# A decoder step in float32: all of the sample's mLSTM state updates moved off TensorE into the MLP, part of them on ScalarE and GpSimd

## The chip, the core and the metric

The kernel runs on one core of a Trainium2 chip. The metric is the device time of one execution in microseconds. The engines are TensorE (PE in the profile, its weight loads PEld), VectorE (DVE), ScalarE (ACT), GpSimd (POOL) and the sync engine (SP), from whose queue nearly all DMAs are started.

## The reference

One layer of a decoder for 320 tokens: a prompt of 256 and a sample of 8 sequences with 8 tokens each (`NP_`, `NB`, `NT`). Two token mixers, an xLSTM mLSTM with 4 heads and an HGRN2 with 8, share one input projection; then come the gates, an output projection, a LayerNorm and an MLP of 2048 to 8192 to 2048 with a squared ReLU. What matters here is the new mLSTM state of each of the 8 sample sequences, an output of 4 heads x 256 x 512 per sequence:

```python
C_new = decay[..., None, None] * C + jnp.einsum('bhs,bhsk,bhsv->bhkv', w_end, kc, vc)
```

So a state row k of a sequence is scaled by one number and receives eight outer-product terms, one for each token s: a scalar (weighted key) times a row of 512 values. The old state C is also read for the output, `einsum('bhtk,bhkv->bhtv', qc, C)`.

## The kernel before

**Weights and TensorE.** Each of some 300 weight tiles (2048 rows x 128 columns) is read in two units of 128 x 1024 numbers. A unit is loaded into `wr` (three buffers, 512 KB each), ScalarE rounds it to the high half `wh`, VectorE subtracts to get the low half `wl`, and TensorE multiplies each of its 8 blocks three times (high x high, high x low, low x high) with 320 columns of activations: 24 matmuls a unit. There are three `wh`/`wl` buffers, and in some stages five more in `bb`. The tiles follow in a fixed order: the mLSTM heads, the HGRN2 heads, gates and branches, `w_out`, and then four rounds of 16 `up` and 16 `dn` tiles of the MLP, which take the last 900 us.

**The order of everything else.** The program is written by a small scheduler (`Sched`). Each piece of work is a generator (a chain) that yields requests such as `("dve", cost, fn)`, `acq` and `rel` for buffers, `wait` and `post` for events. The scheduler keeps a clock per engine out of costs written in the code and puts an instruction on its engine's queue when the clock says that it would be ready. On the chip each queue runs strictly in the order so found. The kind `"bg"` is for background work on VectorE: it is issued only when VectorE's clock is at most 250 ns ahead.

**The sample's states.** For every head, `m_states` loads sixteen pieces of 128 state rows x 512 values (8 sequences x 2 halves of the keys) into `cb` buffers. `m_sample` makes two groups of them. A group first does some small sums (`m_few`), whose results ScalarE copies out of PSUM, then eight products of queries and states. For the first half of the key rows, `m_sums` multiplies `kst` and `vst` (the sample's weighted keys and values, spread over four row groups by broadcast loads and split into high and low parts) into four PSUM banks, one sequence each; `m_update` adds them on VectorE to the scaled state, and `m_store` writes it back.

The second half of the key rows is updated late, in the MLP, when the five buffers in `bb` are given up at the twelfth `up` tile (`retire`). `m_late` reads, for each head, the values of the eight tokens (`vsD`, broadcast to 16 partitions per sequence), the weighted keys (`kD`) as scalars per partition, and the decay (`scr`). A partition is a sequence and one of 16 blocks of 8 key rows; a piece (`m_late_part`) is two of the eight rows, 128 x 1024 values, loaded again from `C0`. ScalarE scales a piece by the decay, then VectorE does 16 operations (8 tokens x 2 rows) of the kind state = value row x key scalar + state, each 128 x 512, and the piece is stored. Four pieces a head, one head after the other, all in a tile called `fu`. When the last head is done, `late_end` gives the space to the prompt's final states (`m_C`), whose loads stand on GpSimd's queue.

Of the kernel before, what the change touches and what calls it, by code (L numbers as in the profile page):

```python
# [8 lines left out]
F32 = mybir.dt.float32  # L9
# [142 lines left out]
class Sched:  # L152
    PE_SIDE = 900.0
    BG = 250.0

# [17 lines left out]
    def step(self, c, now):  # L173
# [27 lines left out]
        else:  # L201
# [6 lines left out]
            if kind == "bg":  # L208
                if (r > now and c.eng != kind) or self.t["dve"] > now + self.BG:
# [11 lines left out]
            end = self.use("dve" if kind == "bg" else kind, r, cost)  # L221
# [86 lines left out]
class Program:  # L308
# [49 lines left out]
    def carve(self):  # L358
# [39 lines left out]
        self.kst = Pool([R.three(2, 128)])  # L398
        self.vst = Pool([R.three(2, 512)])
# [515 lines left out]
    def m_start(self, h):  # L915
# [19 lines left out]
        for name, evs, pool in (("qk", ("dn", "KS", "QW"), self.qk), ("eb", ("N", "S0"), self.eb), ("shl", ("N", "S0"), self.shl),  # L935
                                ("vhl", ("N",), self.vhl), ("vs", ("S0", "vst"), self.vs), ("kst_", ("QW", "KS"), self.kst), ("vst_", ("QW", "vst"), self.vst)):
# [98 lines left out]
    def m_Vs(self, h):  # L1035
# [6 lines left out]
        vst = yield acq(self.vst)  # L1042
        m["vst_"] = vst
        yield from self.sample_rows(self.vtD[h][:, NP_:TOK], vs, vst, self.khl, m["Vs"], m["vst"])

    def sample_rows(self, of, vs, vst, pool, both, four):
# [6 lines left out]
        for j in range(n):  # L1053
# [8 lines left out]
        yield wait(d)  # L1062
        for g in range(2):
# [30 lines left out]
    def m_KW(self, h):  # L1094
# [29 lines left out]
        kst = yield acq(self.kst)  # L1124
        m["kst_"] = kst
        yield from self.fourfold(self.kD[h][256:320, 0:128], kst)
        t = yield acq(self.khl)
        yield from self.high_low(kst.rearrange("p g k -> p (g k)"), t[:, 0:256], 0)
        yield rel(self.khl, t)
# [127 lines left out]
    def m_sample(self, h):  # L1257
# [18 lines left out]
        for k in range(2):  # L1276
# [119 lines left out]
    def m_done(self, h, name, evs, pool):  # L1396
# [3 lines left out]
        if name in ("kst_", "vst_"):  # L1400
            yield wait(*m["inter"])
# [22 lines left out]
    def m_sums(self, h, n, ps):  # L1424

        m = self.mh[h]
        kst, vst = m["kst_"], m["vst_"]
        g = self.state(n)[0] // 4
        for x in range(4):
            self.mm(ps[x], kst[32 * x:32 * x + 32, g, :], vst[32 * x:32 * x + 32, g, :], start=True, stop=True)  # L1430

    def m_update(self, h, n, cbs, ps):

        v, m = self.nc.vector, self.mh[h]
        b = self.state(n)[0]
        for x in range(4):
            yield post(m["inter"][n + 4 + x])
            yield rel(self.cb, cbs[4 + x])
        for x in range(4):
            cb, p, bx = cbs[x], ps[x], b + x  # L1440
            t = yield ("dve", dve(512, True, 1, 1), lambda: v.scalar_tensor_tensor(cb, cb, m["bc"][:, 704 + bx:705 + bx], p, ALU.mult, ALU.add))
            self.s.spawn(self.m_store(h, n + x, cb), 3, t)
            yield rel(self.sbank, p)

    def m_store(self, h, n, cb):
        m = self.mh[h]
        yield ("sp", 620, lambda: self.dma(self.d["Cs"][h, 0, self.state(n)[0]], cb))
        yield post(m["inter"][n])
        yield wait(self.later(2500))
        yield rel(self.cb, cb)  # L1450

    def retire(self, now, hl):

        self.spare.append(hl)
        if len(self.spare) == len(self.wx):
            A = self.Part(self.pool.tile([128, 10240], F32, name="fu", tag="f1"))
            self.lv, self.lc, self.lk = (Pool([]) for _ in range(3))
            self.lv.free = [(now, A.three(4, 512)) for _ in range(2)]
            self.lc.free = [(now, A(1024)) for _ in range(5)]
            self.lk.free = [(now, A(80)) for _ in range(2)]  # L1460
# [3 lines left out]
    def m_late(self, h):  # L1464

        if h:
            yield wait(self.late_ev[h - 1])
        v = yield acq(self.lv, 2)
# [3 lines left out]
        yield ("sp", 620, lambda: self.dma(k[:, 64:65], at(self.scr[h, 704:712].unsqueeze(1))))  # L1472
        for t in range(NT):
            yield wait(self.later(1500))
            x = self.kD[h][NP_:TOK, 128:256].rearrange("(b t) (d r) -> t b d r", t=NT, r=8)[t]
            yield ("sp", 620, lambda: self.dma(k[:, 8 * t:8 * t + 8], x))
        for i in range(4):
            yield wait(self.later(5000))
            x = self.vsD[h].rearrange("(b t) n -> b (t n)", t=NT)[:, 1024 * i:1024 * i + 1024]
            yield ("sp", 620, lambda: self.dma(v[i // 2][:, 2 * (i % 2):2 * (i % 2) + 2, :].rearrange("p t n -> p (t n)"), at(x)))  # L1480
        e = self.later(12000)
        evs = [Ev() for _ in range(4)]
        for q, x in enumerate(evs):
            self.s.spawn(self.m_late_part(h, q, v, k, e, x), 9, e.t + 8000.0 * q - 7000.0)
        yield wait(*evs)
        for x in v:
            yield rel(self.lv, x)
# [976 lines left out]
```

## Time and profile before

| | |
|---|---|
| time, median of three runs | 2244.96 us (2244.36 to 2246.15) |
| the profiled execution | 2246.38 us |
| its span, first to last instruction | 2244.6 us |
| granted TensorE clock | 0.999 |
| busy: PE, PEld, DVE, ACT, POOL | 2236.5, 2208.9, 1583.6, 1029.5, 21.1 us |
| DMA, mean over the span | 200 GB/s |

Rows of groups read: line, engine, operation, tiles written <- tiles read, shapes, count, then busy time in us, mean duration of one in ns, and the idle time of the engine just before them with what ended it. Timeline rows read: start in us from the span's start, busy us, engine and instruction, with the idle time ahead of it in brackets. The names in the profile leave out buffer numbers: `ra` holds `kst` and `vst`, `f` and `rx` the `cb` buffers and more, `bank` a PSUM bank. L352 is the helper that issues all matmuls, L346 the one for all ScalarE operations, L1512 the late update.

### The profile page before, as it was taken

The numbers are of one execution on the slowest core, as the hardware profiler recorded it, in microseconds if no ns is written. First come the engines' busy times: TensorE is split into PE (matmuls) and PEld (weight loads), VectorE is DVE, ScalarE is ACT, GpSimd is POOL, SyncE is SP. The second block draws the span as 40 slices with busy tenths as digits, with TensorE's granted clock in tenths as the row PEclk, the third lists the DMA queues.
The fourth block names the chain that finished last, engine by engine and source line by source line (L and its number), as shares of the span: only waits on it lengthen the run. The fifth ranks groups of instructions, "written<-read, shape, count | busy, mean of one in ns | idle before, by whom it ended". The sixth has DMA issues, their size and how long they took to land.

```text
span 2244.6 us, 40808 instructions
## 1 busy us (share of the span) xinstructions
PE 2236.5 (100%) x16186; PEld 2208.9 (98%) x16186; DVE 1583.6 (71%) x2808; ACT 1029.5 (46%) x1543; POOL 21.1 (1%) x53
## 2 busy tenths in 40 slices
PE   9999999999999999999999999999999999999999
PEld 9999999999999999999999999999999999999998
DVE  6757667789888887666555778368595885944575
ACT  5445445455555565444434456233443444334444
POOL 0000000000000000000000000000000000000000
PEclk9999999999999999999999999999999999999999
DMA  7987987777778765555556544375656657554654
GB/s 247 293 242 242 247 252 232 208 225 214 218 232 236 216 191 176 174 173 172 174 173 217 182 147 153 112 229 181 208 196 180 214 185 210 187 194 150 211 171 148
DMA packets 293145, 449.50 MB, mean 200 GB/s; under 512 B 141508, under 2 KB 187856, under 8 KB 292952
## 3 DMA queue, kind: packets, MB, share of 16 engines
q1 hardware_dynamic: 291992, 443.73, 63.4%
q0 software_dynamic: 960, 3.15, 0.4%
q8 instruction: 127, 2.08, 0.4%
q14 instruction: 66, 0.54, 0.1%
HBM read 397.44 MB, written 49.87 MB: 199 GB/s over the span
## 4 chain that ended last, share of the span: by engine, by line
PE 99%; DMA 0%; ACT 0%; DVE 0%; issue 0%; SPq 0%; DVEq 0%
PE bank L352 99%; DMA f<-xw 0%; ACT wh L346 0%; ACT f L346 0%; SPq L355 0%; ACT misc L346 0%; DVE wh L779 0%; DVE f L2130 0%; DVE f3m L2305 0%; DVE f2l L2129 0%; DVE oS L1896 0%; ACT oS L346 0%; DVEq L1896 0%
## 5 line engine op out<-in xcount | busy, mean ns | idle before, releaser
L346 ACT ACTIVATE wh<-wr 128x1024 fp32r<-128x1024 f32 x563 | 596.6, 1060 | 886.9 <-PE bank L352 789.3
L523 DVE TENSOR_TENSOR wl<-wr,wh 128x1024 fp32r<-128x1024 f32 x563 | 688.1, 1222 | 354.0 <-ACT wh L346 347.4
L352 PE MATMUL bank<-xh,wl 128*128 128x320 f32 (+1 forms) x2896 | 894.6, 310 | 0.0
L352 PE MATMUL bank<-xh,wh 128*128 128x320 f32 (+1 forms) x2896 | 893.5, 309 | 0.5 <-DVE wh L779 0.5
L352 PE MATMUL bank<-xl,wh 128*128 128x320 f32 (+1 forms) x2896 | 890.8, 309 | 0.0
L352 PEld LDWEIGHTS bank<-xh,wh 128*128 128x128 f32 x2896 | 544.2, 188 | 3.8 <-issue 2.0
L352 PEld LDWEIGHTS bank<-xl,wh 128*128 128x128 f32 x2896 | 543.8, 188 | 1.9
L352 PEld LDWEIGHTS bank<-xh,wl 128*128 128x128 f32 x2896 | 545.2, 188 | 0.0
L352 PE MATMUL bank<-ra,wh 128*128 128x320 f32 x1728 | 470.9, 308 | 0.0
L352 PE MATMUL bank<-rxb,wh 128*128 128x320 f32 x1024 | 315.7, 308 | 0.0
L352 PE MATMUL bank<-rxb,wl 128*128 128x320 f32 x1024 | 315.6, 308 | 0.0
L352 PEld LDWEIGHTS bank<-ra,wh 128*128 128x128 f32 x1728 | 309.9, 188 | 0.0
L352 PEld LDWEIGHTS bank<-rxb,wl 128*128 128x128 f32 x1024 | 192.2, 188 | 0.0
L352 PEld LDWEIGHTS bank<-rxb,wh 128*128 128x128 f32 x1024 | 192.2, 188 | 0.0
L1512 DVE SCALAR_TENSOR_TENSOR fu<-fu 128x512 f32<-128x512 f32 x256 | 179.9, 749 | 0.0
L352 PE MATMUL bank<-bb,wh 128*128 128x320 f32 x512 | 112.6, 309 | 0.0
L352 PE MATMUL bank<-ra,wl 128*128 128x320 f32 x352 | 108.5, 308 | 0.0
L346 ACT ACTIVATE f<-bank 128x320 f32<-128x320 f32 (+3 forms) x86 | 33.9, 394 | 114.6 <-PE bank L352 113.6
L352 PEld LDWEIGHTS bank<-bb,wh 128*128 128x128 f32 x512 | 85.5, 188 | 0.0
L346 ACT ACTIVATE f<-f,misc 128x320 f32<-128x320 f32 x136 | 76.2, 560 | 7.0 <-DVE f L2286 3.8
L352 PE MATMUL bank<-bb,wl 128*128 128x320 f32 x256 | 79.1, 309 | 0.0
L346 ACT ACTIVATE f<-f 128x320 f32<-128x320 f32 (+1 forms) x138 | 62.3, 452 | 16.2 <-DVE f L2291 12.3
(345 smaller groups left out, 1916.0 us busy)
## 6 DMA issues: line engine op xcount, KB each, us to landing
wr<-wt SPq DMA_DIRECT2D x602, 512.0 KB
rx<-C SPq DMA_DIRECT2D x34, 256.0 KB
fu<-vsD SPq DMA_DIRECT2D x16, 512.0 KB
fu<-C SPq DMA_DIRECT2D x16, 512.0 KB
Cs<-fu SPq DMA_DIRECT2D x16, 512.0 KB
f<-C SPq DMA_DIRECT2D x30, 256.0 KB
Cs<-f SPq DMA_DIRECT2D x16, 256.0 KB
Cs<-rx SPq DMA_DIRECT2D x16, 256.0 KB
```

The source lines that it names most:

```text
L346: return self.nc.scalar.activation(out, in_, func, **kw)
L352: self.nc.tensor.matmul(*a, **kw)
L523: self.V().tensor_tensor(lo, raw, hi.bitcast(F32), ALU.subtract)
L1512: yield ("bg", dve(512, False, 1, 1), lambda: self.nc.vector.scalar_tensor_tensor(cb[:, r], x, y, cb[:, r], ALU.mult, ALU.add))
```

## The change

The first half of the key rows is no longer updated in the mLSTM stage: `m_sums`, `m_update`, `m_store`, `kst` and `vst` go, with the loads and splits that feed them. The group on TensorE ends after its products with the states, the small sums get a bank of their own, and the group no longer waits for `kst` and `vst`. Instead `m_late` makes eight pieces per head, four for each half of the keys. Pieces 1, 3 and 5 are done without VectorE: ScalarE writes value row x key scalar into one of three buffers (`lp`), and GpSimd adds it to the state. A new kind `"bga"` holds back such ScalarE work as `"bg"` does on VectorE. There are three value buffers (half a head each) instead of two, so a piece may begin when the first four tokens' values are there, four piece buffers instead of five, and the next head starts its loads as soon as the last one's have been issued. The head's first four pieces are spaced only for head 0; otherwise the scheduler fits them in where its clocks allow.

```diff
+    LOW = dict(bg="dve", bga="act")
...
-            yield wait(m["KS"], m["vst"], m["S"])
+            yield wait(m["S"])
             dn = yield acq(self.sm)
-            ps = yield acq(self.sbank, 4)
-            t = yield ("pe", PE_C + PE_4 + pe_r(512) + 200.0, lambda: (
-                self.m_few(m, k, ps[3], dn, self.qn0[:, lo:lo + 128]), [self.mm(
+            p = yield acq(self.sbank)
+            yield ("pe", PE_C + 200.0, lambda: (
+                self.m_few(m, k, p, dn, self.qn0[:, lo:lo + 128]), [self.mm(
...
-                start=k == 0 and c == 0, stop=False, skip_group_check=True) for c in range(2) for x in range(4)], self.m_sums(h, 8 * k, ps)))
-            self.s.spawn(self.m_update(h, 8 * k, cbs, ps), 3, t)
+                start=k == 0 and c == 0, stop=False, skip_group_check=True) for c in range(2) for x in range(4)]))
+            yield rel(self.sbank, p)
...
-            self.lv.free = [(now, A.three(4, 512)) for _ in range(2)]
-            self.lc.free = [(now, A(1024)) for _ in range(5)]
+            self.lv.free = [(now, A.three(4, 512)) for _ in range(3)]
+            self.lc.free = [(now, A(1024)) for _ in range(4)]
+            self.lp.free = [(now, B(512)) for _ in range(3)]
...
+                for q in range(8):
+                    s.spawn(self.m_late_part(h, q, v, k, got, half[q], done[q]), 9, now + 6000.0 * q if h == 0 and q < 4 else now)
...
+        yield ("bga", act(1024, False, 1), lambda: self.A(buf, buf, scale=k[:, 128:129]))
...
+                if q % 2 and q < 6:
+                    p = yield acq(self.lp)
+                    yield ("bga", act(512, False, 1), lambda: self.A(p, x, scale=y))
+                    evs.append(Ev())
+                    self.s.spawn(self.m_late_add(cb[:, r], p, evs[-1]), 9)
+                else:
+                    yield ("bg", dve(512, False, 1, 1), lambda: self.nc.vector.scalar_tensor_tensor(cb[:, r], x, y, cb[:, r], ALU.mult, ALU.add))
...
+    def m_late_add(self, x, p, ev):
+
+        yield ("pool", 1000, lambda: self.nc.gpsimd.tensor_tensor(x, x, p, ALU.add))
+        yield rel(self.lp, p)
+        yield post(ev)
```

How the order moves is shown at three places. First, TensorE at the first state group of head 0, before (`misc<-` in a bank's row are the small sums, `f_79` and `rx` the states, `ra` with 512 columns the products of `kst` and `vst`, the other rows weight matmuls):

```order
L352 MATMUL bank_83<-xh,wl 128x320
L352 MATMUL bank_86<-misc,f_78 32x1 x8
L352 MATMUL bank_86<-f_76 32x32 x4
L352 MATMUL bank_87<-f_79 32x512 x6
L352 MATMUL bank_87<-rx,f_79 32x512 x2
L352 MATMUL bank_89<-ra 128x512
L352 MATMUL bank_90<-ra 128x512
L352 MATMUL bank_85<-ra 128x512
L352 MATMUL bank_86<-ra 128x512
L352 MATMUL bank_83<-xh,wh 128x320
```

The same place after the change:

```order
L353 MATMUL bank_83<-xh,wl 128x320
L353 MATMUL bank_89<-misc,f_78 32x1 x8
L353 MATMUL bank_89<-f_76 32x32 x4
L353 MATMUL bank_87<-f_79 32x512 x6
L353 MATMUL bank_87<-rx,f_79 32x512 x2
L353 MATMUL bank_83<-xh,wh 128x320
```

The four products are gone, of which the last wrote the bank of the small sums (`bank_86`); the group stands 72 rows earlier, and so it goes at all eight groups.

Second, VectorE in the MLP, while a head's late update runs, before (`wl<-wr,wh` is the split of a weight unit, `fu<-fu` the late update, the 320-wide rows are evacuations of the MLP's tiles):

```order
L523 TENSOR_TENSOR wl<-wr,wh 128x1024
L1512 SCALAR_TENSOR_TENSOR fu<-fu 128x512 x4
L523 TENSOR_TENSOR wl<-wr,wh 128x1024
L1512 SCALAR_TENSOR_TENSOR fu<-fu 128x512
L2291 SCALAR_TENSOR_TENSOR f_78<-bank_84,f2l 128x320
L1512 SCALAR_TENSOR_TENSOR fu<-fu 128x512 x2
```

And after:

```order
L522 TENSOR_TENSOR wl<-wr,wh 128x1024
L1488 SCALAR_TENSOR_TENSOR fu<-fu,f_78 128x512 x3
L522 TENSOR_TENSOR wl<-wr,wh 128x1024
L1488 SCALAR_TENSOR_TENSOR fu<-fu,f_78 128x512
L2297 TENSOR_TENSOR f3m<-f3m,bank_87 128x320
L1488 SCALAR_TENSOR_TENSOR fu<-fu,f_78 128x512 x2
```

The pattern is the same, three late rows a unit. What moved is how long it lasts: before, stretches of this kind (some 20 units, one per head) alternate with stretches without late rows, from unit 396 to unit 532 of 602; after, it runs without a break from unit 398 to unit 502, 320 rows instead of 256.

Third, ScalarE at the same time after the change, with the semaphores that each row waits for (before, its rows there are weight splits `wh<-wr`, evacuations and one `fu<-fu 128x1024` per piece):

```order
L347 ACTIVATE wh<-wr 128x1024 [waits DMAHW3_49,DVE_49,PE_49]
L347 ACTIVATE f_78<-fu,f_78 128x512 [waits Pool_49] x4
L347 ACTIVATE wh<-wr 128x1024 [waits DMAHW6_49,DVE_49,PE_49]
L347 ACTIVATE f_78<-fu,f_78 128x512 [waits Pool_49] x4
L347 ACTIVATE wh<-wr 128x1024 [waits DMAHW1_49,DVE_49,PE_49]
L347 ACTIVATE f_78<-fu,f_78 128x512 [waits Pool_49] x3
```

Up to four products now stand between two weight splits, and each waits until GpSimd has added the product that held its buffer. GpSimd's queue has one row for all of them, `TENSOR_TENSOR fu<-fu,f_78 128x512 x192`, ahead of the loads for `m_C`.

More of the change, by code (lines that the diff above doesn't have):

```diff
@@ L220, in step @@
                 return False
-            end = self.use("dve" if kind == "bg" else kind, r, cost)
+            end = self.use(self.LOW.get(kind, kind), r, cost)
             fn()
@@ L1052, in sample_rows @@
         e = self.later(5000)
-        for j in range(n):
+        for j in range(n if vst is not None else 0):
             for g in range(2):
@@ L1061, in sample_rows @@
         yield post(both)
-        yield wait(d)
-        for g in range(2):
+        if vst is not None:
+            yield wait(d)
+        for g in range(2 if vst is not None else 0):
             yield from self.high_low(vst[:, g, :], t[:, 0:128 * n], 1)
```

123 lines of the change are left out of this document (51 added, 72 removed).

## Prediction

> **What bounds the kernel now.** I read the page's totals first, then the chain that ended last, then the stages.
>
> ```profile
> span 2244.6 us, 40808 instructions
> PE 2236.5 (100%) x16186; PEld 2208.9 (98%) x16186; DVE 1583.6 (71%) x2808; ACT 1029.5 (46%) x1543; POOL 21.1 (1%) x53
> ...
> PE 99%; DMA 0%; ACT 0%; DVE 0%; issue 0%; SPq 0%; DVEq 0%
> ```
>
> TensorE (PE) works in 2236.5 of 2244.6 us, and the chain is 99% TensorE. So two things alone can move the time: TensorE instructions that vanish, and TensorE made to wait. Everything else is covered, as long as the cover lasts. Whether it lasts is read by stage (columns: PE, PEld, DVE, ACT, POOL busy us and count, clock, DMA share, GB/s):
>
> ```profile
> 1500.00:1550.00 50.00, 50.00 (x342) 50.00 (x342) 49.85 (x69) 16.44 (x16) 0.00 (x0) 1.00 0.58 197
> ...
> 90.00:400.00 310.00, 308.99 (x2203) 293.41 (x2200) 208.07 (x409) 144.96 (x235) 0.00 (x0) 1.00 0.82 244
> ```
>
> In the MLP, where one head of the late states is being updated, VectorE is already full (49.85 of 50 us) without TensorE losing anything; 342 matmuls in 50 us are 0.1462 us each. ScalarE is a third busy, GpSimd idle. The average of 71% for VectorE hides this.
>
> **What leaves TensorE.** These are timeline rows of TensorE at three of the eight state groups, in the mLSTM stage (start, us, instruction):
>
> ```profile
> 90.20 0.50 PE L352 MATMUL bank<-ra 32*128 32x512 f32 x3
> 91.33 0.50 PE L352 MATMUL bank<-ra 32*128 32x512 f32 x1 [0.64 <-ACT misc L346]
> 91.76 0.41 PE L352 MATMUL bank<-xh,wh 128*128 128x320 f32 x1
> ...
> 99.86 0.51 PE L352 MATMUL bank<-ra 32*128 32x512 f32 x4
> 100.30 0.41 PE L352 MATMUL bank<-xh,wh 128*128 128x320 f32 x1
> ...
> 178.62 0.50 PE L352 MATMUL bank<-ra 32*128 32x512 f32 x3
> 179.49 0.49 PE L352 MATMUL bank<-ra 32*128 32x512 f32 x1 [0.37 <-ACT misc L346]
> ```
>
> The four 32-row products of a group run side by side: from the first of them to the next weight matmul 100.30 - 99.86 = 0.44 us, and 8 x 0.44 = 3.5 us. At two groups the fourth product also waits until ScalarE has copied the small sums out of the same bank: 91.33 - 90.20 = 1.13 and 179.49 - 178.62 = 0.87 us, 2.0 us together. After the change the small sums have a bank of their own and nothing follows in it. So TensorE gains 5.5 us; the bounds are 3.5 (the copies delay something else) and 5.5. The 32 PSUM updates on VectorE, twelve high/low passes on each of ScalarE and VectorE, and 40 broadcast loads leave the same stage; VectorE has 102 us free there and TensorE waits about 1 us in all, so I cost them at nothing. The groups of head 0 now come some ten microseconds earlier; their state loads move up with them, since the broadcasts that stood between them on the sync queue are gone. I cost that at nothing (bounds: 0, and one late load of about 1 us, as the waits above).
>
> **What comes into the MLP.** Per head eight pieces instead of four. From the order: 320 products-and-sums on VectorE instead of 256, 32 ScalarE scalings instead of 16, and new: 192 ScalarE products with 192 GpSimd additions. All of it stands between the weight splits of units 398 and 503, where before it reached unit 532. That is 105 units of 24 matmuls, 2520 x 0.1462 = 368.4 us of TensorE. VectorE's rows:
>
> ```profile
> L1512 DVE SCALAR_TENSOR_TENSOR fu<-fu 128x512 f32<-128x512 f32 x256 | 179.9, 749 | 0.0
> ...
> L2305 DVE TENSOR_TENSOR f3m<-f3m,bank 128x320 f32<-128x320 f32 x36 | 17.5, 486 | 15.4 <-PE bank L352 15.0
> ```
> ```profile
> 1505.61 2.07 DVE L1512 SCALAR_TENSOR_TENSOR fu<-fu 128x512 f32<-128x512 f32 x3
> 1507.60 1.22 DVE L523 TENSOR_TENSOR wl<-wr,wh 128x1024 fp32r<-128x1024 f32 x1
> 1508.74 0.75 DVE L1512 SCALAR_TENSOR_TENSOR fu<-fu 128x512 f32<-128x512 f32 x1
> ```
>
> Durations overlap, so the step from start to start is what counts when VectorE is full: (1507.60 - 1505.61)/3 = 0.663 us, 1.14 us for a weight split, and by the same 0.085 us of overlap 0.40 us for a 320-wide row. In the stretch: 320 x 0.663 = 212.2, 105 x 1.14 = 119.7, 81 x 0.40 = 32.4, together 364.3 us of 368.4. It fits, with 4 us to spare over the whole stretch, where before the same stretch held 276 us. What lead there is beyond that shows in the longest wait of ScalarE's split for a free buffer:
>
> ```profile
> ACT wh L346 <- PE bank L352: 790.0, 407, 5.4
> ```
>
> About 5 us. So VectorE can lose 4 + 5 = 9 us in this stage before TensorE stands still, and with the 5.5 us gained, 14.5 us before the kernel is slower than it was. Spread over 192 additions this is 0.075 us each. That number decides the sign.
>
> ScalarE: 192 products; the nearest row, with a scale per partition and 512 columns, has 718 ns.
>
> ```profile
> L346 ACT ACTIVATE ra<-ra,cst 128x512 fp32r<-128x512 f32 x12 | 8.6, 718 | 1.7 <-DVE ra L1143 1.7
> ...
> L346 ACT ACTIVATE fu<-fu 128x1024 f32<-128x1024 f32 x16 | 18.2, 1139 | 0.3 <-DMA fu<-C 0.2
> L346 ACT ACTIVATE wh<-wr 128x1024 fp32r<-128x1024 f32 x563 | 596.6, 1060 | 886.9 <-PE bank L352 789.3
> ```
>
> 192 x 0.72 = 138, 32 x 1.14 = 36, 105 x 1.06 = 111 and 56 evacuations of 0.5, 28: 313 of 368 us. It fits by itself, but ScalarE takes its queue in order, and behind each product that waits for one of three GpSimd buffers stands the next weight split. Transfers: 16 loads and 16 stores of 512 KB more, in 370 instead of 476 us, make (80 x 0.524 MB)/370 us = 113 GB/s instead of 53: 197 + 60 = 257 GB/s, near the 244 at a share of 0.82 that cost TensorE 1 us in 310. Nothing, bound 3 us. The 64 short key loads instead of 32 and the 32 large transfers add some 64 issues of 0.6 us to the sync queue, which mostly waits for VectorE: nothing. GpSimd's queue has the twelve loads for the prompt states behind the additions; those are wanted 100 us later (before, the last late row ran at 1964 us; the new place is unit 502, near 1860 us). The library instruction that GpSimd runs ahead of its first scaling now stands ahead of its first addition, and GpSimd has been idle for long there: nothing.
>
> **GpSimd's additions.** No row shows such an addition. The nearest:
>
> ```profile
> L2346 POOL TENSOR_SCALAR f3m<-f3m,vec 128x320 f32<-128x320 f32 x7 | 4.3, 612 | 120.2 <-ACT f3m L346 114.7 <-DVE f3m L2327 4.5 <-ACT oC L346 1.0
> ...
> L710 POOL MEMSET f<- 128x512 f32 x1 | 0.5, 530 | 0.0
> L711 POOL COPY f<-f 128x128 f32<-128x128 f32 x1 | 0.4, 382 | 11.7 <-DMA f<-wif 11.7
> ```
>
> From 128 to 320 columns with one input, (612 - 382)/192 = 1.2 ns a column: 0.84 us for 512, the low bound; twice that, 1.68 us, for two inputs, the high one. The memset's 530 ns for a single pass says that the low end is nearer, and I take 1.1 us. The Trainium skill, "GPSIMD Engine Reference", section on performance versus the Vector engine, has 2.6 cycles a column for this addition at 1.2 GHz, an estimate of 1.11 us; the sum goes by the bounds from the rows.
>
> What does it do to VectorE meanwhile? There is one place where GpSimd read SBUF beside VectorE rows with two SBUF inputs (VectorE, then GpSimd, then ScalarE):
>
> ```profile
> 12.41 0.49 DVE L756 TENSOR_TENSOR xl<-f,xh 128x320 fp32r<-128x320 f32 x1
> 12.82 0.56 DVE L756 TENSOR_TENSOR wl<-f,wh 128x384 fp32r<-128x384 f32 x1
> 13.38 0.50 DVE L756 TENSOR_TENSOR xl<-f,xh 128x320 fp32r<-128x320 f32 x1
> ```
> ```profile
> 13.15 0.38 POOL L711 COPY f<-f 128x128 f32<-128x128 f32 x1 [11.74 <-DMA f<-wif]
> ```
> ```profile
> 12.87 0.47 ACT L346 ACTIVATE xh<-f 128x320 fp32r<-128x320 f32 x1
> ```
>
> The copy began inside the 0.56 us row, took 0.38 us for a quarter of the memset's columns, and ended after that row had; the next VectorE row started 0.56 us later, though ScalarE's input for it (12.87 + 0.47 = 13.34) explains that start. So it fits taking turns, and it fits no contact at all: it bounds the delay at 0 to 0.08 us for a tiny copy. An addition reads eight times as many values. The likeliest mechanism: a VectorE row with two SBUF inputs and a GpSimd row that reads SBUF take turns. Then 320 x 0.663 + 105 x 1.14 + 28 x 0.40 = 343 us of VectorE and 192 x 1.1 = 211 us of GpSimd must fit one after the other into 368.4 + 5 us: 343 + 211 - 373 = 181 us of standing TensorE; less 5.5, +175 us. Bounds: at 0.84 us per addition +125, at 1.68 us, with the 53 PSUM evacuations not overlapped either (21 us), +308 us. The Trainium skill says this outright ("SBUF — State Buffer", who interferes with whom): VectorE's second SBUF input goes through the read port that is GpSimd's only one, and whichever comes second waits for the whole instruction. By that page the sum is the same 175 us; without it, the 0.075 us threshold is what I would lean on, and still expect a loss.
>
> **The rivals.**
> 1. Taking turns instruction by instruction, as above: 2244.96 + 175 = 2420 us. For it: the copy's 0.38 us. Against it: that row can be read otherwise.
> 2. Partial turns: VectorE loses half of each addition, 0.55 us. Then 364 + 106 - 373 = 97, less 5.5: 2336 us. Deciding point again 0.075 us.
> 3. No contact, everything covered, the other sign: 2244.96 - 5.5 = 2239.5 us, 0.24% faster. For it: 364.3 us fit into 368.4, and the copy did not visibly stretch its neighbours (0.50 against 0.49 us).
> 4. No contact, but ScalarE waits for GpSimd: in the densest ten units the order has 32 products in 35 us, so additions over 1.1 us fall behind; at 1.3 us by 6.5 us, against 5 us of lead, in about three such stretches. 2240 to 2248 us.
> 5. The gain eaten by small stalls of VectorE at 99% load: within 0.2%.
>
> **How the numbers follow.** The profiled execution took 2246.38 us, its span 2244.6; the median of three is 2244.96, and I add to that. 0.2% (4.5 us) is about what a measurement can tell from no change. Chances: first 0.57, second 0.18, third 0.14, fourth 0.06 (half slower, half within), fifth 0.05. Slower 0.57 + 0.18 + 0.03 = 0.78, within 0.03 + 0.05 = 0.08, faster 0.14. The first case's own range is 2370 to 2553. The range given, 2242 to 2520, leaves out the third case and additions above about 1.6 us.
>
> **What the profile after would show.** Right: the 32x512 products and the two ScalarE waits gone from TensorE, 5.5 us; the late rows done in VectorE's order by unit 502; products-and-sums of well over 0.75 us or gaps between them where a GpSimd addition runs; TensorE idle behind weight splits in about 1490 to 2030 us and nowhere else; GpSimd additions of 1 to 2 us. Wrong: VectorE steps of 0.66 us kept beside additions, which leaves rivals three to five, told apart by whether ScalarE's products wait for GpSimd.

## The result, and the profile after

The changed kernel takes 2432.54 us (median of four executions, 2431.44 to 2433.48) against 2244.82 us: a ratio of 1.0833, 95% interval [1.0818, 1.0849], 187.7 us slower. The forecast was 2420 us. The profiled execution has a span of 2429.4 us and a granted clock of 0.976.

The page's totals, and the chain that ended last by engine and by line:

```profile
span 2429.4 us, 41289 instructions
PE 2290.4 (94%) x16154; PEld 2251.0 (93%) x16154; DVE 1791.3 (74%) x2828; ACT 1163.5 (48%) x1739; POOL 369.6 (15%) x245
...
PE 78%; DVE 17%; issue 4%; DMA 1%; ACT 0%; SPq 0%; DVEq 0%; ACTq 0%
PE bank L353 78%; DVE fu L1488 11%; DVE wl L522 5%; DMA wr<-wt 1%; DVE ra L1974 1%; DMA f<-xw 0%; DVE f L2283 0%; DVE f3m L2297 0%; ACT wh L347 0%; SPq L356 0%; DMA f<-kD 0%; DVE wh L778 0%; DVE f L2122 0%; DVE f2l L2121 0%; DVE oS L1888 0%
```

TensorE bounded 99% of the chain; now it is 78%, and 16% lies with two VectorE lines: the late rows (L1488) and the weight splits (L522). TensorE is still busy for 94% of the span, so the totals alone would still call it the bound. The stage tells more. Three stretches of after, in the columns of the prediction's stage table (PE, PEld, DVE, ACT, POOL, clock, DMA share, GB/s), and then the stretch of the late rows as one:

```profile
1400.00:1480.00 80.00, 80.00 (x548) 80.00 (x547) 29.70 (x34) 23.38 (x28) 0.00 (x0) 1.00 0.45 129
1600.00:1700.00 100.00, 70.78 (x438) 68.19 (x439) 100.00 (x92) 52.88 (x75) 63.87 (x35) 0.93 0.51 165
2050.00:2150.00 100.00, 100.00 (x684) 100.00 (x683) 46.09 (x52) 34.12 (x37) 4.59 (x6) 1.00 0.54 179
```

```profile
1492.00:2052.00 560.00, 427.23 (x2525) 413.30 (x2524) 557.20 (x507) 290.95 (x388) 348.59 (x192) 0.90 0.52 170
```

Ahead of the late rows and behind them TensorE loses nothing. Between 1492 and 2052 us VectorE is busy for 557.20 of 560 us, and TensorE for 427.23. The same rows were to take 364.3 us. The groups of GpSimd's additions and of VectorE's late rows (busy us, mean ns):

```profile
L1499 POOL TENSOR_TENSOR fu<-fu,f 128x512 f32<-128x512 f32 x192 | 348.6, 1849 | 947.1 <-ACT f L347 947.1
...
L1488 DVE SCALAR_TENSOR_TENSOR fu<-fu,f 128x512 f32<-128x512 f32 x320 | 364.8, 1182 | 0.0
```

An addition lasts 1849 ns on the average, a late row 1182 instead of 749. The timeline shows how, VectorE first and then GpSimd, in the same stretch:

```profile
1563.98 2.06 DVE L1488 SCALAR_TENSOR_TENSOR fu<-fu,f 128x512 f32<-128x512 f32 x3
1565.97 1.21 DVE L522 TENSOR_TENSOR wl<-wr,wh 128x1024 fp32r<-128x1024 f32 x1
...
1569.49 1.21 DVE L522 TENSOR_TENSOR wl<-wr,wh 128x1024 fp32r<-128x1024 f32 x1
1570.63 6.91 DVE L1488 SCALAR_TENSOR_TENSOR fu<-fu,f 128x512 f32<-128x512 f32 x4
```

```profile
1569.38 7.60 POOL L1499 TENSOR_TENSOR fu<-fu,f 128x512 f32<-128x512 f32 x4 [11.20 <-ACT f L347]
```

Without GpSimd three late rows take 2.06 us. When ScalarE has filled its buffers and four additions run, the next four late rows take 6.91 us, 1.73 each, and the four additions 7.60, 1.90 each: one pair at a time. The minimum, median and maximum of three forms of VectorE row over the whole execution say which rows this befalls:

```profile
L1488 DVE SCALAR_TENSOR_TENSOR fu<-fu,f x320: 732/743/1795, 1492.6 to 2051.3; 128x512 f32<-128x512 f32 x160
```

```profile
L1974 DVE TENSOR_TENSOR ra<-f,rxb x64: 476/484/1584, 794.7 to 2294.9; 128x320 fp32r<-128x320 f32 x64
```

```profile
L2297 DVE TENSOR_TENSOR f3m<-f3m,bank x64: 468/486/490, 1434.1 to 2405.8; 128x320 f32<-128x320 f32 x64
```

The 320-wide sum with both inputs in SBUF (`f,rxb`) goes from 484 to as much as 1584 ns; the equally wide one that reads a PSUM bank never exceeds 490. To size it, I sorted the VectorE rows of this stage by whether a GpSimd instruction of the late update overlaps them (mean ns, count in brackets), here and in two of the experiments below:

| VectorE row | alone, after | beside additions, after | beside copies | beside memsets |
|---|---|---|---|---|
| late row, 512 columns, two SBUF inputs | 739 (167) | 1665 (153) | 1018 (158) | 750 (218) |
| weight split, 1024 columns, two SBUF inputs | 1213 (52) | 1947 (59) | 1460 (62) | 1225 (74) |
| `ra` sum, 320 columns, two SBUF inputs | 478 (12) | 966 (18) | 699 (17) | 489 (19) |
| evacuation, 320 columns, one input in PSUM | 478 (26) | 477 (5) | 478 (10) | 488 (19) |

So the additions lengthened VectorE's work by 153 x 0.926 + 59 x 0.734 + 18 x 0.488 = 194 us, 1.01 us for each of the 192. Undisturbed 364 and these 194 make 558, the 557.2 that the stage shows. Who waits for that: TensorE for weight splits; and ScalarE's products for GpSimd. The last line is VectorE's only wait in that stage:

```profile
PEld bank L353 <- DVE wl L522: 144.5, 51, 6.9
PE bank L353 <- DVE wl L522: 131.1, 48, 6.7
...
ACT f L347 <- POOL fu L1499: 66.0, 75, 1.6
```

```profile
DVE wl L522 <- ACT wh L347: 8.7, 3, 5.9
```

TensorE's gaps can also be followed back in the trace, each from the delayed matmul to what released it, then to what that waited for or stood behind. Of the 64 gaps of over 0.25 us that TensorE has in this stage (145 us), 61 (139 us) lead into VectorE's own queue of late rows and splits, and the others to DMAs.

The part of the change in the mLSTM stage is there as well. TensorE at the first group of states of head 0, where the four `ra` products and the wait for ScalarE had stood:

```profile
86.55 0.31 PE L353 MATMUL bank<-xh,wl 128*128 128x320 f32 x1
86.79 0.24 PE L353 MATMUL bank<-misc,f 128*32 128x1 f32 x8
86.87 1.46 PE L353 MATMUL bank<-rx,f 128*32 128x512 f32 x10
...
88.17 0.60 PE L353 MATMUL bank<-f 128*32 128x512 f32 x2
88.70 0.41 PE L353 MATMUL bank<-xh,wh 128*128 128x320 f32 x1
```

The next weight matmul follows the last state products 0.5 us later. By the start of unit 380's weight split the changed kernel is 4.6 us ahead of the one before, and then loses it many times over.

### The profile page after: what moved, and what is told of

The parts are those of the page before. It is cut to its first block, busy times and chain, and to the rows that moved or that the text cites. A ratio compares the mean times of both kernels' runs of the same rounds, so it can differ in the third digit from the quotient of the medians.

```text
span 2429.4 us, 41289 instructions
## 1 busy us (share of the span) xinstructions
PE 2290.4 (94%) x16154; PEld 2251.0 (93%) x16154; DVE 1791.3 (74%) x2828; ACT 1163.5 (48%) x1739; POOL 369.6 (15%) x245
## 3 DMA queue, kind: packets, MB, share of 16 engines
q8 instruction: 126, 2.06, 0.4%
## 4 chain that ended last, share of the span: by engine, by line
PE 78%; DVE 17%; issue 4%; DMA 1%; ACT 0%; SPq 0%; DVEq 0%; ACTq 0%
PE bank L353 78%; DVE fu L1488 11%; DVE wl L522 5%; DMA wr<-wt 1%; DVE ra L1974 1%; DMA f<-xw 0%; DVE f L2283 0%; DVE f3m L2297 0%; ACT wh L347 0%; SPq L356 0%; DMA f<-kD 0%; DVE wh L778 0%; DVE f L2122 0%; DVE f2l L2121 0%; DVE oS L1888 0%
## 5 line engine op out<-in xcount | busy, mean ns | idle before, releaser
L353 PE MATMUL bank<-xh,wl 128*128 128x320 f32 (+1 forms) x2896 | 908.3, 315 | 71.4 <-DVE wl L522 71.2
L522 DVE TENSOR_TENSOR wl<-wr,wh 128x1024 fp32r<-128x1024 f32 x563 | 730.1, 1297 | 324.5 <-ACT wh L347 321.4
L353 PE MATMUL bank<-xh,wh 128*128 128x320 f32 (+1 forms) x2896 | 903.7, 313 | 1.0 <-DVE wh L778 1.0
L353 PE MATMUL bank<-xl,wh 128*128 128x320 f32 (+1 forms) x2896 | 901.1, 312 | 0.0
L1499 POOL TENSOR_TENSOR fu<-fu,f 128x512 f32<-128x512 f32 x192 | 348.6, 1849 | 947.1 <-ACT f L347 947.1
L353 PE MATMUL bank<-ra,wh 128*128 128x320 f32 x1728 | 480.8, 314 | 0.6 <-DVE ra L1974 0.6
L1488 DVE SCALAR_TENSOR_TENSOR fu<-fu,f 128x512 f32<-128x512 f32 x320 | 364.8, 1182 | 0.0
L353 PE MATMUL bank<-rxb,wl 128*128 128x320 f32 x1024 | 325.6, 318 | 40.4 <-DVE wl L522 40.4
L347 ACT ACTIVATE f<-fu,f 128x512 f32<-128x512 f32 x192 | 133.4, 715 | 66.3 <-POOL fu L1499 66.0
L353 PEld LDWEIGHTS bank<-ra,wl 128*128 128x128 f32 x352 | 67.2, 191 | 22.1 <-DVE wl L522 22.1
```

What stands on the lines that cost most here:

```text
L347: return self.nc.scalar.activation(out, in_, func, **kw)
L353: self.nc.tensor.matmul(*a, **kw)
L522: self.V().tensor_tensor(lo, raw, hi.bitcast(F32), ALU.subtract)
L1488: yield ("bg", dve(512, False, 1, 1), lambda: self.nc.vector.scalar_tensor_tensor(cb[:, r], x, y, cb[:, r], ALU.mult, ALU.add))
L1499: yield ("pool", 1000, lambda: self.nc.gpsimd.tensor_tensor(x, x, p, ALU.add))
```

## Experiments

The runs are compared with the kernel before on the same chip (2244.4 to 2245.8 us, median). This table follows VectorE's part of a unit's weight split through the program: how much later (us) it starts than in the trace of before.

| unit | after | memsets 1.37 us | one memset 0.53 us | all on VectorE | all on VectorE, spread | thinner |
|---|---|---|---|---|---|---|
| 380 | -4.6 | -5.7 | -6.1 | -5.8 | -5.3 | -5.7 |
| 398 | -1.4 | +1.2 | -1.2 | -0.4 | -6.4 | -6.7 |
| 440 | +93.5 | +21.5 | +6.5 | +0.2 | -2.4 | -6.4 |
| 500 | +190.2 | +46.6 | +16.5 | +8.8 | +5.3 | -5.2 |
| 560 | +185.8 | +41.8 | +12.6 | +10.5 | +7.7 | -5.6 |
| 595 | +186.1 | +41.8 | +12.6 | +6.8 | +3.6 | -0.9 |

**Does what GpSimd reads matter, or how long it is busy?** Three memsets of the product's buffer in place of each addition; the order of the program is otherwise the same. In this and the two next runs the products are not added to the state.

```diff
-        yield ("pool", 1000, lambda: self.nc.gpsimd.tensor_tensor(x, x, p, ALU.add))
+        yield ("pool", 1000, lambda: [self.nc.gpsimd.memset(p, 0.0) for _ in range(3)])
```

> The changed kernel with three GpSimd memsets of the product's buffer (3 x 0.53 us, writes only) in place of each addition; the additions are left out of the states of three pieces in eight. GpSimd is as busy per product as with an addition, ScalarE's products still wait for it. Taking turns over the read side: VectorE's late rows stay at 0.75 us beside the memsets, 2238 to 2246 us. ScalarE waiting for GpSimd is the cause (rival): still 2300 us or more. Any GpSimd access to SBUF excludes VectorE (second rival): 3 x 0.5 x 192 = 290 us of turns, 2500 us.

Measured: 2303.1 us, 1.0263 [1.0248, 1.0278]. VectorE's late rows take 744 ns beside a memset and 743 alone, so the reading matters for VectorE, as said. But the time did not go back to before: 58 us are lost without any turn, and 2303 is the time that the first rival, ScalarE waiting for GpSimd, had called for. Two shorter lengths were tried, to see whether GpSimd's queue does this.

```diff
+        yield ("pool", 1000, lambda: [self.nc.gpsimd.memset(p[:, 0:n], 0.0) for n in (512, 512, 256)])
```

> Each GpSimd addition is replaced by memsets of 512, 512 and 256 columns of the product's own buffer, about 1.28 us together, the time that an addition took with no late VectorE row in the program; they write and read nothing. So GpSimd's queue is as long as with undisturbed additions, but it reads no SBUF. Theory 1 (two separate costs: ScalarE's products wait for GpSimd's queue, and VectorE and GpSimd take turns): the queue alone is left; with three full memsets (1.57 us) it cost 58 us, so 1.28 us should cost about half, 2265 to 2285. VectorE's rows unstretched (0.74 and 1.22 us beside GpSimd's work). Theory 2 (all of the loss comes from turns; the 58 us belonged to the longer memsets alone): 2240 to 2250.

Measured: 2286.4 us, 1.0185 [1.0172, 1.0199], just above the first theory's range. The late rows (minimum, median, maximum), and two waits of ScalarE between 1350 and 2150 us:

```profile
L1488 DVE SCALAR_TENSOR_TENSOR fu<-fu,f x320: 735/748/780, 1495.2 to 1907.6; 128x512 f32<-128x512 f32 x160
```

```profile
ACT wh L347 <- DMA wr<-wt: 70.8, 28, 7.1
ACT f L347 <- POOL f L1499: 34.6, 61, 1.2
```

No late row exceeds 780 ns. GpSimd's work per product is 2 x 0.528 + 0.312 = 1.37 us, as long as an undisturbed addition or a little longer, and the time is 146 us below that of the changed kernel: this is what the reading costs. 41.7 us stay. What of them is GpSimd's queue (61 waits of ScalarE, 34.6 us) the next run tells.

```diff
+        yield ("pool", 1000, lambda: self.nc.gpsimd.memset(p, 0.0))
```

> Each addition is replaced by one memset of 512 columns of the product's buffer, 0.53 us, writes only: the order of the changed kernel with a GpSimd that is always done before ScalarE's next product. If the 42 to 61 us that the runs with 1.37 and 1.58 us of memsets per product lost came from ScalarE waiting for GpSimd's queue, it goes, and what is left is the burst of late loads: 2243 to 2255. If they came from ScalarE's 192 products themselves or from VectorE's order (364 us of work in 368), it stays at 2270 to 2290.

Measured: 2259.15 us, 1.0068 [1.0054, 1.0081], somewhat above the first theory's range and well below the second's. So 0.53, 1.37 and 1.58 us of GpSimd per product give 2259, 2286 and 2303 us: a queue of GpSimd behind which ScalarE waits, and with it the weight splits behind the product, costs time by itself, 27 us from the first to the second. The order had planned 1.0 us. The 14.6 us that stay with a GpSimd that is never late come mostly with weight loads: ScalarE waits 69.8 us for them between 1350 and 2150 us, 26.5 in before (below), and 10 of TensorE's 15 gaps of over 0.25 us (8 of 12 us) lead back to one. Three lead to VectorE's own queue.

**One input instead of two.** The product is copied over the state's piece instead of added (the old state and the other terms are lost there).

```diff
+        yield ("pool", 1000, lambda: self.nc.gpsimd.tensor_copy(x, p))
```

> Each addition is replaced by a GpSimd copy of the product to the state's piece: one SBUF operand is read instead of two. If every GpSimd row that reads SBUF takes turns with VectorE's two-input rows (the theory of the prediction), the scalar_tensor_tensor rows beside it are stretched by about the copy's own length, 0.6 to 1.0 us each: 192 x 0.6 to 1.0 = 115 to 190 us less the 10 or so that the order has to spare, 2340 to 2430. If only rows with two SBUF inputs on both sides meet, VectorE's rows are not stretched (0.74 us) and the time is 2240 to 2285.

Measured: 2304.4 us, 1.0265 [1.0252, 1.0278], between the two theories' ranges. Late rows and copies (minimum, median, maximum):

```profile
L1488 DVE SCALAR_TENSOR_TENSOR fu<-fu,f x320: 732/745/1166, 1490.6 to 1921.9; 128x512 f32<-128x512 f32 x160
...
L1499 POOL COPY fu<-f x192: 613/1070/2243, 1498.0 to 1890.6; 128x512 f32<-128x512 f32 x192
```

The rows are stretched, so a GpSimd row with one SBUF input does take turns, but by 0.28 us and not by the copy's whole 0.613 us. The sum over the table's column is 158 x 0.276 + 62 x 0.243 + 17 x 0.216 = 62 us. On top of 364 us it makes 426, against 368 and a lead of 5: 53 lost, less the 5.5, +48; measured +59.7. The 12 us between are not assigned; ScalarE waits only 6.6 us for GpSimd here.

**GpSimd's additions without VectorE's late rows.** The 320 rows are left out, all products and additions stay.

```diff
-                    yield ("bg", dve(512, False, 1, 1), lambda: self.nc.vector.scalar_tensor_tensor(cb[:, r], x, y, cb[:, r], ALU.mult, ALU.add))
+                    pass
```

> The changed kernel without VectorE's 320 late rows (five pieces in eight are only scaled); all 192 ScalarE products and GpSimd additions stay. Taking turns with VectorE as the full engine: VectorE has 152 us of work and 192 x 1.03 = 198 us of turns for 368 us, so it fits: 2239 to 2248 us, though a weight split beside an addition still takes about 2 us instead of 1.22; the additions get shorter than 1.74 us, near 1.4. ScalarE waiting for GpSimd (rival): products still wait, and it stays well above 2260 us. Overload of VectorE by late rows alone (rival): 2239 to 2248 too, so this run tells only the ScalarE rival.

Measured: 2334.25 us, 1.0395 [1.0382, 1.0409]: far above the range for turns, and where the rival, ScalarE waiting for GpSimd, had put it. The additions, the weight splits that are left beside them, and ScalarE's wait for GpSimd (total us, times, longest):

```profile
L1499 POOL TENSOR_TENSOR fu<-fu,f x192: 1260/1298/2302, 1504.6 to 1838.5; 128x512 f32<-128x512 f32 x192
```

```profile
L522 DVE TENSOR_TENSOR wl<-wr,wh x563: 1149/1226/2328, 26.2 to 2299.3; 128x1024 fp32r<-128x1024 f32 x188
```

```profile
ACT f L347 <- POOL fu L1499: 69.7, 83, 1.7
```

114 of the additions take about 1.3 us: that is an addition's own time. Beside a weight split it is 2.3, and the splits there take 1818 ns on the average (67 of them) against 1225 alone. VectorE was busy for only 190 of the 400 us from 1500 to 1900, and TensorE still lost 57: a weight split that is held late costs TensorE its time at once, however much room VectorE has over the stage. What held it here was mostly GpSimd's queue: 49 of TensorE's 61 gaps of over 0.25 us (53 of 69 us) lead back, through a weight split on ScalarE, to a product that waited for an addition. Without the late rows the order had packed the additions closer, between units 400 and 470 instead of 494. So this run mixes the queue with the turns between additions and weight splits, and sizes neither.

**The same instructions with the prices that were measured.** The order counts 1.75 us for an addition and 0.6 us more for a late row. The 35 late rows that run after unit 574 read factors from a buffer that the next stage has begun to load into by then, so some state rows come out different; instructions and shapes are those of the changed kernel.

```diff
-                    yield ("bg", dve(512, False, 1, 1), lambda: ...
+                    yield ("bg", dve(512, False, 1, 1) + 600.0, lambda: ...
...
-        yield ("pool", 1000, lambda: self.nc.gpsimd.tensor_tensor(x, x, p, ALU.add))
+        yield ("pool", 1750, lambda: self.nc.gpsimd.tensor_tensor(x, x, p, ALU.add))
```

> The changed kernel with the order's prices set to what was measured: 1.75 us for an addition instead of 1.0, and 0.6 us more for each of VectorE's 320 late rows. The same instructions, spread from unit 398 to the last, 602, instead of 502. VectorE's work there is 552 us by undisturbed durations and about 194 more by turns, 746 in 719 us. If turns fill VectorE's time, what does not fit is lost: 27 us less 5.5, plus 5 to 15 for late loads, 2265 to 2290. If additions cost TensorE their time wherever they stand (a port or queue that TensorE's own work needs), the loss stays near that of the change, 2400 to 2440.

Measured: 2337.97 us, 1.0416 [1.0400, 1.0432], between the theories. In the stage of the additions:

```profile
1500.00:1900.00 400.00, 370.37 (x2449) 363.29 (x2447) 370.33 (x346) 222.32 (x292) 210.11 (x116) 0.99 0.58 192
1900.00:2160.00 260.00, 236.34 (x1532) 231.71 (x1533) 236.04 (x217) 138.14 (x181) 133.31 (x76) 0.97 0.56 181
```

VectorE is no longer full on the average (370 of 400, 236 of 260 us), and yet TensorE stood for 30 and 24 us there. At unit 595 this version is 71 us behind; the other 22 of its 93 us come after that, where the last late rows (to 2293 us) hold up the end. Spreading halves the loss. What is left is again the single split that is held up, but not by the same queue as in the run before: 44 of TensorE's 47 gaps of over 0.25 us (58 of 63 us) lead into VectorE's own queue, where a split stands behind late rows that additions stretch.

**Everything on VectorE.** No ScalarE products, no GpSimd; 512 late rows.

```diff
-                if q % 2 and q < 6:
+                if False:
```

> All eight pieces of a head go to VectorE; no ScalarE products, no GpSimd additions. VectorE then has 512 late rows at 0.663 us in its order between weight units 398 and 561, with the splits and evacuations 576 us of work for 575 us of TensorE. Taking turns (a VectorE row with two SBUF inputs and a GpSimd row that reads SBUF exclude each other): nothing is left to take turns with, so the 5.5 us of TensorE come out, less a few us because VectorE is full: 2239 to 2246 us. Plain overload of VectorE (the rival: the late rows themselves were too many): at least as slow as the changed kernel, 2430 us or more. The late rows should keep 0.75 us each.

Measured: 2249.96 us, 1.0022 [1.0013, 1.0031], 4 us above the first range and nowhere near the rival's; the late rows take 740 ns. The 5.8 us gained in the mLSTM stage are there (table), and 11 us of the time are lost after it. ScalarE's wait for weight loads between 1350 and 2150 us, in before and here (total us, times, longest):

```profile
ACT wh L346 <- DMA wr<-wt: 26.5, 8, 4.6
```

```profile
ACT wh L347 <- DMA wr<-wt: 120.8, 48, 8.0
```

**The mLSTM part alone**, with the second half of the keys on VectorE as before; the first half is not updated.

```diff
-                for q in range(8):
+                for q in range(4, 8):
...
-                if q % 2 and q < 6:
+                if False:
```

> The mLSTM part of the change alone: the 32 products and the groups' shared bank go from TensorE, and the MLP has the four pieces of the second half per head on VectorE as before (the first half of the key rows is left without its update). No GpSimd additions. It measures the gain that the change was costed with: 5.5 us, 2239.5 us, ratio 0.9975; bounds 3.5 to 6 us. If the earlier groups made TensorE wait for state loads, the gain would be below 3.5 us.

Measured: 2259.04 us (2251.64 to 2265.2 in six executions), 1.0061 [1.0045, 1.0076], not the 2239.5 that was expected. The gain is 5.5 us at unit 380; at unit 460 the version is 22.9 us behind. The same wait of ScalarE:

```profile
ACT wh L347 <- DMA wr<-wt: 109.0, 30, 11.1
```

ScalarE stands up to 11.1 us for a weight load while the four pieces of a head and its values, in loads of 512 KB, come in one burst. So the loads were spread:

```diff
-            yield wait(self.later(4500))
+            yield wait(self.later(9000))
             x = self.vsD[h]...
...
-                    s.spawn(self.m_late_part(...), 9, now + 6000.0 * q if h == 0 and q < 4 else now)
+                    s.spawn(self.m_late_part(...), 9, now + 8000.0 * (q - 4))
```

> The mLSTM part of the change alone with the four pieces of the second half on VectorE, as in the run that gave 2259 us; the loads of the sample's values are issued 9 us apart instead of 4.5, the pieces of the keys 8 us apart instead of at once. First half of the keys is not updated. If that run lost its 20 us because a burst of late loads held the MLP's weight loads, most of it comes back: 2239 to 2244, ScalarE's splits wait no longer for weight loads than before. If it lost them for another reason (VectorE's 256 rows, the store of the pieces), it stays at 2255 to 2262.

Measured: 2246.62 us (2241.1 to 2254.09 in twelve executions), 1.0009 [1.0000, 1.0017], between the two ranges. Over the kernel before on the same chip, 14.6 us became 1.9. So of the 20.1 us lost (14.6 and the 5.5 gained), 12.7 came back by moving the loads, and with them the rows that use them (the last late row at 1831 instead of 1801 us); the burst was the larger part of the loss. That ScalarE would wait no longer for weight loads than before did not come true in the trace (100.6 us against 26.5), which is of the slowest of the twelve executions. The wide spread of the times suggests that what is left depends on how transfers fall in each execution; no run tests it.

**A version with everything on VectorE and spread loads.**

```diff
-                if q % 2 and q < 6:
+                if False:
...
-            yield wait(self.later(4500))
+            yield wait(self.later(9000))
             x = self.vsD[h]...
...
-                    s.spawn(self.m_late_part(...), 9, now + 6000.0 * q if h == 0 and q < 4 else now)
+                    s.spawn(self.m_late_part(...), 9, now + 7000.0 * q if h == 0 else now)
```

> All eight pieces on VectorE, no GpSimd work, and the late loads spread: values 9 us apart, pieces of the first head 7 us apart. All of the computation is kept. If the 2250 us of the unspread version were 5.6 us gained in the mLSTM stage and 12 us lost to bursts of loads, this gives 2238 to 2243 and beats the kernel before by 2 to 6 us. If VectorE's 512 rows themselves cost the 12 us (its order is full there: 576 us of work in 575 us), it stays at 2247 to 2253.

Measured: 2248.87 us, 1.0018 [1.0009, 1.0027]: in the second theory's range, but not by its cause. Spreading gave back only about 1 us here, yet the loss still comes with weight loads. ScalarE's wait for weight loads, and one such wait in the timeline of TensorE and ScalarE:

```profile
ACT wh L347 <- DMA wr<-wt: 106.4, 44, 10.6
```

```profile
1717.70 0.31 PE L353 MATMUL bank<-rxb,wh 128*128 128x320 f32 x1
1717.99 0.31 PE L353 MATMUL bank<-rxb,wl 128*128 128x320 f32 x1
1719.36 1.06 ACT L347 ACTIVATE wh<-wr 128x1024 fp32r<-128x1024 f32 x1 [10.59 <-DMA wr<-wt]
...
1720.47 0.64 PE L353 MATMUL bank<-rxb,wh 128*128 128x320 f32 x1 [2.17 <-ACT wh L347]
...
1720.90 0.47 PE L353 MATMUL bank<-ra,wh 128*128 128x320 f32 x1
...
1721.73 0.64 PE L353 MATMUL bank<-rxb,wl 128*128 128x320 f32 x1 [0.36 <-DVE wl L522]
...
1722.43 0.47 PE L353 MATMUL bank<-ra,wh 128*128 128x320 f32 x1
1722.69 0.47 PE L353 MATMUL bank<-rxb,wl 128*128 128x320 f32 x1
```

ScalarE waited 10.59 us for one weight load, TensorE 2.17 us; then weight matmuls start 0.26 us apart (1722.43, 1722.69) instead of 0.145, for about 5 us. Over 1450 to 2150 us such gaps cost 5.5 us and the slow starts 3.3, together the 8.8 us by which this version lost. Of the 8 gaps of over 0.25 us, 7 lead back to a weight load and one to VectorE's own queue.

**Thinner.** The spread version, in which a late row is issued only where VectorE's order has 0.2 us free. As above, rows after unit 574 (41 here) read factors that have been replaced.

```diff
-    BG = 250.0
+    BG = -200.0
```

> All eight pieces on VectorE, late loads spread as in the run that gave 2249 us, and a late row is placed only where VectorE's order has 0.2 us free (instead of up to 0.25 us behind): 651 us of work over 705 us to the last unit, instead of 577 in 575. All of the computation is kept. If that run's loss came from weight loads behind a dense stream of late loads and stores, the thinner stream gives back most: 2239 to 2245, the best of the versions. If late loads hurt wherever they stand, 2247 to 2252.

Measured: 2254.23 us, 1.0039 [1.0027, 1.0052], above both ranges. The stretch of the late rows:

```profile
1500.00:2050.00 550.00, 550.00 (x3756) 550.00 (x3755) 514.13 (x703) 230.86 (x266) 0.00 (x0) 1.00 0.67 216
```

Not a microsecond of TensorE is lost in these 550 us, ScalarE's wait for weight loads is down to 39.1 us, and the whole 5.6 us are kept up to unit 560 (table). The loss comes behind: the last late row runs at 2207 us, and the loads of the prompt's states, which wait for its space, start at 2211 us, in the spread version at 2091. The last version, again from the spread one, ends the rows at unit 573:

```diff
-    BG = 250.0
+    BG = 0.0
...
-        B = self.Part(self.f2, 960)
-        self.sraw = Pool([B(768) for _ in range(3)])
+        B = self.Part(self.f2, 1232)
+        self.sraw = Pool([B(768) for _ in range(2)])
```

> All eight pieces on VectorE, no GpSimd, late loads spread, a late row placed only where VectorE's order is not ahead: 591 us of work over 607 us, units 401 to 573, so that the rows end before the next stage's loads need their factors' buffer (that stage gets two staging buffers behind it instead of three on it). All of the computation is kept. The thinner version kept the whole 5.5 us up to unit 560 and lost them only behind it, where its last rows held up the end. If the density of the late loads and rows alone decides, this one keeps 2 to 5 us: 2239 to 2243, faster than the kernel before. If 97% is as full as 100%, it loses at units 440 to 540 as that version did: 2246 to 2250.

Measured: 2245.48 us, 1.0002 [0.9994, 1.0011], the time of before, between the two ranges. It was 5.2 us ahead at unit 560, so the density theory held that far, and lost it near 2130 us, where ScalarE stood for the next stage's loads (wait of ScalarE, 2090 to 2150 us; total, times, longest), with the next weight split queued behind:

```profile
ACT xhs L347 <- DMA f<-sD: 13.7, 3, 8.9
```

No version beat the kernel before: the 5.5 us of the mLSTM stage were given back in the MLP or behind it each time.

## Why the prediction was right, point by point

- **TensorE's gain of 5.5 us.** Right: 4.6 us in the changed kernel and 4.8 to 6.1 in the experiments at unit 380, against bounds of 3.5 to 5.5. All are taken against the one trace of before, whose execution took 1.4 us longer than the median.
- **VectorE's order holds 364 of 368 us.** Right: 557.2 us of work in the trace less 194 of stretch are 363.
- **Taking turns, the likeliest case.** Right, and it is shown twice: with GpSimd writing only, as long, the time falls by 146 us and no VectorE row is stretched; with GpSimd reading one operand they are stretched by less. Rows with one PSUM input stay as they were, as the sum had assumed for the evacuations; but it had put all 53 of them beside additions, and only 17 ran there. The Trainium skill, "SBUF — State Buffer", who interferes with whom, names the same pairs, and the traces agree on them; it also has the second instruction wait for the whole of the first, and there they differ (last section).
- **The addition at 1.1 us.** Two misjudgements that cancel: an addition by itself takes 1.28 to 1.30 us, inside the bounds of 0.84 and 1.68, and it holds VectorE for 1.01 us, four fifths of its length. So the turns are not whole, but nearer to the first case than to the half of rival 2. With 1.28 us and whole turns the sum would have given 2455 us, so the nearness of 2420 is in part luck. With the measured terms the sum is 364 + 194 of work and 3 idle, less 373: 188 instead of 181, and with the 4.6 us gained 2428 us. The 4 us that are left are about the lead of 5 that was assumed; whether it was there is not resolved.
- **Rival 4, ScalarE waiting for GpSimd, at most 8 us.** Undersized. With turns excluded it was worth about 27 us at 1.37 us per product and 44 at 1.58 (2286 and 2303 less 2259). The prediction counted three dense stretches; an order that plans 1.0 us for what takes more is late in all of them. In the changed kernel itself this wait (66.0 us) adds nothing that shows: VectorE is full, stood only 8.7 us for ScalarE, and no gap of TensorE leads back to it.
- **Transfers: "Nothing, bound 3 us".** Wrong. The mean rate over the stage did not show it: with bursts of 512 KB loads ScalarE stood up to 11 us for a weight load, and spreading them gave back 12.7 us in the mLSTM part alone, and about 1 us with everything on VectorE. The changed kernel hides this too. Most weight loads are not issued late: in before, in both dense versions with everything on VectorE and in both of the mLSTM part alone, nine in ten start within 0.04 us of their buffer's release, the rest up to 5.3 us after it. But of those that ScalarE waited for, the longest took 10.5 us from issue to landing in before, 12.9 in the spread version and 18.0 in the mLSTM part alone. Whether that is the rate or the order in which transfers are served was not told apart.
- **Where TensorE would stand.** Right: idle behind weight splits from about 1492 to 2040 us and nowhere else.

The rivals without contact rested on the small copy beside a 0.56 us row, which had fitted both; the likeliest case rested on turns. What the prediction did not see is that its other covers were gone as well: without GpSimd, none of the four versions that did all the updates on VectorE was faster.

## What to carry to other kernels

Before work is moved to an idle GpSimd, look at what the VectorE rows beside it read: if both inputs are in SBUF and GpSimd reads SBUF, the two engines are nearly one resource (here an addition of 1.28 us cost VectorE 1.01), and their times have to fit together into the stage. When an order is planned from prices, an engine that is given too low a price delays not its own work but the queue of whoever waits for it: here 1.37 us of memsets planned as 1.0 held weight splits and cost 27 us. And a gain upstream is only kept if the stage that receives the work has room in its transfers too, burst by burst and not on the average.

## What the runs showed of the hardware

- The pair is not served strictly one after the other. A late row (0.74 us) and an addition (1.28 alone) together take 1.74 us, the median of the additions, 0.28 less than their sum; a late row and a copy (0.61 alone) 1.07, again 0.28 less. The late row delays GpSimd by 0.46 us in both; the addition delays the row by 0.93, the copy by 0.28.
- TensorE can pay for a gap a second time. Behind some gaps weight matmuls start 0.27 us apart instead of 0.146 for 3 to 6 us; in the spread version the granted clock is 0.50 from 1722 to 1727 us, behind its gap of 2.17 us. In the changed kernel 398 starts between 1450 and 2150 us are of this kind, 49 us beside 141 for the gaps, which is most of why TensorE's busy time rose from 2236.5 to 2290.4 us with less to do, and the granted clock of the stage fell to 0.90; with 1.37 us of memsets it is 11 us beside 36. The Trainium skill, "TensorE: Matmul & The Clock Gate", part on the clock gate, has the half rate after an idle window of about 3.4 us; here the gap of 2.17 us was enough: the two matmuls right behind it (1720.47 and 1720.90) are already slow.
